# Routing per token tile, and the expert lists sorted in two unequal parts

## The chip, the cores and the metric

The kernel runs on one core of a Trainium2 chip. The metric is the device time of one execution in microseconds (us), lower is better. TensorE multiplies matrices, VectorE and ScalarE do the elementwise work, GpSimd (POOL) some of it and the indirect transfers, SyncE (SP) issues the other transfers. Each engine works through its own queue in order; semaphores join them.

## The reference

Two transformer-like blocks stand one behind the other. The change touches the end of the first and a preparation of the second. The first block's mixed features (1024 tokens x 1024) go through the output projection; the result is normalised, gated, added to the residual, normalised again to h, and h goes to a mixture of experts in which the experts choose: each of the 16 experts takes the 128 tokens (`cap`) with the highest softmax probability for it.

```python
affinity = jax.nn.softmax((h @ w_router).astype(jnp.float32), axis=-1)
gate_vals, tok_idx = lax.top_k(jnp.swapaxes(affinity, 1, 2), cap)
xs = jax.vmap(lambda hb, ib: hb[ib])(h, tok_idx)
```

Behind it the experts' gated MLPs run over `xs` and are added back to the tokens. The second block needs, among other things, columns of constants and an LRU constant (softplus of a parameter, by a series of small operations), and the keys and values of a memory of 256 tokens.

## The kernel before, in words

`first` calls `phase_out`, `phase_topk`, `setup2` and `phase_moe1`. A scheduler orders the instructions afterwards, so that pieces of these stand among each other in the engines' queues.

`phase_out` works in four blocks of two token tiles (128 tokens each). `gates(blk)` prepares a block's left factors: it loads the retention rows (`lt`), transposes them (`ltp`), loads the RWKV rows (`gy`), normalises them (`gyn`), transposes (`yT`) and gates them; high and low parts are split (`lTh`, `lTl`). The loop calls `gates` for the next block and then, for both tiles of a block, the projection (`mo`, 48 matmuls for each tile through `mm3`), a copy by ScalarE, `row_norm` (a square with a sum on ScalarE, scaling on VectorE, a power on POOL), the residual and a second `row_norm`, giving `h` (L1094, L1095), which is stored to `h2d`. `route(t, h2)` runs one tile late: 8 transpositions (`h2p`), 8 small matmuls for the logits (`rl`), a copy into a table of all tiles (`routlg`).

After the last tile one softmax over the whole table is made (L1103 to L1108), 8 matmuls against the identity (`pa`) turn it, and one copy (L1112) puts it into `affT`: 64 partitions x 512, the first 512 tokens for each expert on rows 0 to 15, the others on rows 32 to 47. `phase_topk` then runs 16 rounds of three VectorE instructions over 512 columns: the eight largest (L1127), their positions (L1128, a load of the values and a search), and their replacement by -1 (L1130). Both halves have then their 128 best in order; one merge (L1133 to L1144) keeps the larger of the first list and the reversed second one, which leaves the 128 best of all. Two transpositions (`tkps`) and two copies give the gate values `gv` and the token numbers `idx`.

`setup2` loads 88 columns of constants for the second block (`c3`, transposed through a PSUM tile), runs `phase_mem` (256 memory tokens: square, scaling, transposition `memT`, projection `mkv`, normalisation on POOL, transposition `mkT`), `lru_consts` (L1324 to L1340, 27 VectorE operations of 128x8 named `sp`, `cl`, `ncl`) and `rope_setup` (the load `posi`, its cast `posf`, the angles `ang`).

`phase_moe1` loads the weights of expert after expert in pieces of 1 MB (`m1r`), 14 of them ahead; the 15th load waits for the first gather (`xg`, an indirect transfer by `idx`, L1200). The pieces are split into `m1h` and `m1l`; the gathered tokens are transposed (`xT0p`) and multiplied (`gu`, `dn`).

## Time and profile before

| | |
|---|---|
| time, median of 3 runs | 4141.37 us (4128.83 to 4142.38) |
| profiled execution | 4133.8 us |
| its span in the trace | 4132.0 us |
| mean granted TensorE clock | 0.951 |
| PE busy | 3779.7 us (91%) |
| DVE busy | 2814.2 us (68%) |
| ACT busy | 2127.7 us (51%) |
| POOL busy | 825.2 us (20%) |

PE is TensorE, DVE VectorE, ACT ScalarE, SP SyncE. Busy shares are means over stages with different limits; the stretch of the change is read from windows and timelines, with times in us from the span's start. A granted clock of 1.00 is 2.4 GHz, 0.50 is 1.2 GHz. Durations in a row are those of one instruction, or of a run of xN instructions; L12 is line 12 of the kernel.

### The profile page before, as it was taken

Reading aid. Unit: us, or ns where it says so; the run is one execution under the profiler, and the core shown is the slowest. Engines: PE = TensorE matmul, PEld = TensorE weight load, DVE = VectorE, ACT = ScalarE, POOL = GpSimd, SP = SyncE. Lnnn points to the kernel's source line nnn. Section 1 sums busy time; section 2 is a strip of 40 time slices with the busy share of each in tenths; the row PEclk is TensorE's granted clock in tenths of the full one; section 3 lists DMA queues with packets and bytes.
Section 4 is the critical chain, followed back from the end, with each engine's and each line's share of the span. In section 5 each row is a group of like instructions: output and inputs, shape, how many; then the busy total and the mean of one; then the engine's idle time right before and its main releaser. Section 6 shows DMA issues by size and latency. Waiting matters only on the chain. (4 is left out here: it accounts for less than half of the span.)

```text
span 4132.0 us, 61749 instructions
## 1 busy us (share of the span) xinstructions
PE 3779.7 (91%) x23138; PEld 3133.2 (76%) x23138; DVE 2814.2 (68%) x4777; ACT 2127.7 (51%) x3389; POOL 825.2 (20%) x1054
## 2 busy tenths in 40 slices
PE   7988887998997879999969999999998999999998
PEld 4877886777875647777747788888886777788876
DVE  3578787776776578888865513676644356799987
ACT  3443322332323347777758712666653244688876
POOL 2333324233224120000010001222210022221111
PEclk7999998998998989999989999999999999899999
DMA  6555455455445379999851122111115425899998
GB/s 229 169 168 163 138 153 142 109 135 129 112 115 177 129 295 374 382 371 385 319 171 46 50 66 66 44 37 42 47 62 167 142 79 204 324 384 386 382 381 303
DMA packets 503961, 782.78 MB, mean 189 GB/s; under 512 B 199697, under 2 KB 334811, under 8 KB 502507
## 3 DMA queue, kind: packets, MB, share of 16 engines
q1 hardware_dynamic: 430314, 631.77, 43.8%
q0 software_dynamic: 40816, 138.37, 11.3%
q10 hardware_dynamic: 32528, 8.66, 0.9%
q8 instruction: 184, 3.01, 0.3%
q14 instruction: 119, 0.97, 0.1%
HBM read 646.28 MB, written 132.43 MB: 188 GB/s over the span
## 5 line engine op out<-in xcount | busy, mean ns | idle before, releaser
L2262 DVE TENSOR_TENSOR m2l<-m2r,m2h 128x1024 fp32r<-128x1024 f32 x380 | 449.6, 1222 | 53.0 <-ACT m2h L2261 48.6
L1195 DVE TENSOR_TENSOR m1l<-m1r,m1h 128x2048 fp32r<-128x2048 f32 x189 | 427.2, 2289 | 72.5 <-ACT m1h L1194 70.6
L2261 ACT CAST m2h<-m2r 128x1024 fp32r<-128x1024 f32 x384 | 394.0, 1050 | 86.5 <-PE m2g L109 34.6
L1194 ACT CAST m1h<-m1r 128x2048 fp32r<-128x2048 f32 x192 | 362.1, 1914 | 111.3 <-PE gu L109 82.6
L108 PE MATMUL m2g<-m2l,m2thx 128*128 128x512 f32 x512 | 202.7, 396 | 1.8 <-DVE m2l L2262 1.3
L107 PE MATMUL m2g<-m2h,m2thx 128*128 128x512 f32 x512 | 202.9, 405 | 0.3 <-ACT m2h L2261 0.3
L109 PE MATMUL m2g<-m2h,m2tlx 128*128 128x512 f32 x512 | 201.5, 394 | 0.0
L108 PE MATMUL gu<-m1l,xh 128*128 128x512 f32 x512 | 199.7, 395 | 0.0
L109 PE MATMUL gu<-m1h,xl 128*128 128x512 f32 x512 | 199.1, 395 | 0.0
L107 PE MATMUL gu<-m1h,xh 128*128 128x512 f32 x512 | 182.4, 397 | 12.7 <-ACT xh L60 8.3
L515 DVE TENSOR_TENSOR tripr<-triN,triX 128x1 f32<-128x1 f32 (+30 forms) x155 | 131.9, 851 | 19.5 <-POOL triX L511 15.9
L107 PE MATMUL apqk<-atW_hi,hT2h 128*128 128x256 f32 x512 | 145.1, 283 | 0.0
L108 PE MATMUL apqk<-atW_lo,hT2h 128*128 128x256 f32 x512 | 144.7, 283 | 0.0
L109 PE MATMUL apqk<-atW_hi,hT2l 128*128 128x256 f32 x512 | 144.7, 283 | 0.0
L107 PE MATMUL u_ps<-hTh,inW_hi 128*128 128x512 f32 (+1 forms) x336 | 127.1, 378 | 2.6 <-ACT u L342 1.5
L2314 POOL DMA_INDIRECT out_dram<-m2y,did x32 | 68.9, 2154 | 302.5 <-ACT m2y L2313 302.5
L108 PE MATMUL u_ps<-hTl,inW_hi 128*128 128x512 f32 (+1 forms) x336 | 124.4, 370 | 0.0
L109 PE MATMUL u_ps<-hTh,inW_lo 128*128 128x512 f32 (+1 forms) x336 | 124.1, 370 | 0.0
L107 PEld LDWEIGHTS gu<-m1h,xh 128*128 128x128 f32 x512 | 95.0, 188 | 37.0 <-ACT xh L60 10.7
L108 PEld LDWEIGHTS gu<-m1l,xh 128*128 128x128 f32 x512 | 96.4, 188 | 27.0 <-DVE m1l L1195 7.4
L1216 POOL DMA_INDIRECT accd<-y,idx x16 | 29.1, 1819 | 435.2 <-ACT y L1215 400.1
L108 PEld LDWEIGHTS m2g<-m2l,m2thx 128*128 128x128 f32 x512 | 96.8, 189 | 24.8 <-DVE m2l L2262 6.1
(1215 smaller groups left out, 11720.3 us busy)
## 6 DMA issues: line engine op xcount, KB each, us to landing
m2r<-in_w_gate_up_dram SPq DMA_DIRECT2D x128, 1024.0 KB
m1r<-in_w_gate_dram SPq DMA_DIRECT2D x64, 1024.0 KB
m1r<-in_w_up_dram SPq DMA_DIRECT2D x64, 1024.0 KB
m1r<-in_w_down_dram SPq DMA_DIRECT2D x64, 1024.0 KB
m2r<-in_w_down_dram SPq DMA_DIRECT2D x64, 1024.0 KB
inW_raw<-in_w_in_dram SPq DMA_DIRECT2D x72, 256.0 KB
m2w<-in_w_mod_dram POOLq DMA_DIRECT2D x32, 512.0 KB, 4.7
luW_raw<-in_w_in_dram SPq DMA_DIRECT2D x24, 512.0 KB
```

Of the source, the lines that this page charges most:

```text
L107: nc.tensor.matmul(ps, lh, rh, start=start, stop=False)
L108: nc.tensor.matmul(ps, lh, rl, start=False, stop=False)
L109: nc.tensor.matmul(ps, ll, rh, start=False, stop=stop)
L515: nc.vector.tensor_mul(pr[:, :m, :m], N[:, j, j + 1:].unsqueeze(1).to_broadcast([P, m, m]), X[:, j + 1:, j + 1:].rearrange("p s t -> p t s"))
L1194: nc.scalar.copy(hi, raw)
L1195: (nc.gpsimd if i < 3 else nc.vector).tensor_sub(lo, raw, hi)
L1216: nc.gpsimd.indirect_dma_start(out=E.accd, out_offset=bass.IndirectOffsetOnAxis(ap=E.idx[:, e:e + 1], axis=0), in_=y, in_offset=None, comp ...
L2261: nc.scalar.copy(hi, raw[:, j])
L2262: (nc.gpsimd if i in (0, 2) else nc.vector).tensor_sub(lo, raw[:, j], hi)
L2314: nc.gpsimd.indirect_dma_start(out=E.x4d, out_offset=bass.IndirectOffsetOnAxis(ap=col, axis=0), in_=y, in_offset=None, compute_op=OP.add)
```

## The change

The blocks of `phase_out` are taken in the order 1, 2, 0, 3, so that tiles 0 to 5 come first and 6 and 7 last. `route` makes the softmax of its own tile (128x16), one `pa` for the tile, and copies its 128 columns to `affA` (tiles 0 to 5, 16x768, rows 0 to 15) or `affB` (tiles 6 and 7, 16x256, rows 32 to 47). `TopK.rounds(part, n)` runs rounds of one part. Six rounds of part 0 are written behind tile 6, six ahead of tile 7's routing, four behind it, and the 16 rounds of part 1 in `phase_topk`; the replacement is made in place. The merge is as before with 768 in place of 512. The columns `c3` and `lru_consts` (now `consts2`) are called in the second block's turn of `phase_out` and use one of its PSUM tiles.

```diff
@@ -43,13 +43,13 @@
     return r
-def load_cols(E, name, srcs):
+def load_cols(E, name, srcs, psum=None):
     nc = E.nc
     n = sum(ap.shape[0] for ap in srcs)
     rows = E.misc.tile([P, P], F32, tag="colrows", name=f"{name}_rows")
     col_rows(nc, rows, srcs)
-    ps = E.ps_small.tile([P, 512], F32, tag="sm", name=f"{name}_ps")
+    ps = psum(name=f"{name}_ps") if psum else E.ps_small.tile([P, 512], F32, tag="sm", name=f"{name}_ps")
     nc.tensor.transpose(ps[:, :n], rows[:n, :], E.ident[:n, :n])
     out = E.const.tile([P, n], F32, name=name)
     nc.scalar.copy(out, ps[:, :n])
@@ -934,7 +934,8 @@
                 others.pop(0)()
-def phase_out(E, A):
+def phase_out(E, A, others, topk):
@@ -1030,7 +1031,8 @@
                     split_hl(E, zv[:, 0], lTh[:, 4 + h + 2 * q], lTl[:, 4 + h + 2 * q])
             return lTh, lTl
-        lT = [gates(0)]
+        ORDER = (1, 2, 0, 3)
+        lT = [gates(ORDER[0])]
         wo = A.w_out[0]
         rw = wo[512:1024].rearrange("(p h v) f -> p h v f", p=NPAIR, h=2)
         wts = []
@@ -1052,9 +1054,9 @@
         sh2 = bc_row(E, rp, 2, "sh2row")
         wr = rp.tile([P, KD, 16], F32, name="wrouter")
         nc.sync.dma_start(wr, A.w_router[0].rearrange("(k p) e -> p k e", p=P))
-        lg = rp.tile([P, 8, 16], F32, name="routlg")
-        lp32 = rp.tile([P, 8, 32], F32, name="routp")
-        nc.vector.memset(lp32, 0.0)
+        lps32 = [rp.tile([P, 32], F32, name=f"routp{i}") for i in range(2)]
+        for l in lps32:
+            nc.vector.memset(l, 0.0)
         def route(t, h2):
             hT = to.tile([P, KD, P], F32, tag="hT", bufs=1, name=f"h2T{t}")
@@ -1066,13 +1068,27 @@
             pl = pt.tile([P, 16], F32, tag="tr", name=f"rl{t}")
             for k in range(KD):
                 nc.tensor.matmul(pl, hT[:, k], wr[:, k], start=(k == 0), stop=(k == KD - 1))
-            nc.scalar.copy(lg[:, t], pl)
+            mx = to.tile([P, 2], F32, tag="mx", name=f"rmx{t}")
+            nc.vector.tensor_reduce(mx[:, 0:1], pl, axis=AX.X, op=OP.max)
+            g = to.tile([P, 16], F32, tag="lg", name=f"routlg{t}")
+            nc.vector.tensor_scalar(g, pl, mx[:, 0:1], None, op0=OP.subtract)
+            nc.scalar.activation(g, g, AF.Exp)
+            nc.vector.tensor_reduce(mx[:, 1:2], g, axis=AX.X, op=OP.add)
+            nc.vector.reciprocal(mx[:, 1:2], mx[:, 1:2])
+            nc.vector.tensor_scalar(lps32[t % 2][:, 0:16], g, mx[:, 1:2], None, op0=OP.mult)
+            pa = pt.tile([P, P], F32, tag="tr", name=f"pa{t}")
+            r0 = 0 if t < 6 else 32
+            nc.tensor.matmul(pa[r0:r0 + 32], lps32[t % 2], E.ident, start=True, stop=True)
+            dst = E.affA[:, t * P:(t + 1) * P] if t < 6 else E.affB[:, (t - 6) * P:(t - 5) * P]
+            nc.vector.tensor_copy(dst, pa[r0:r0 + 16])
         pend = []
-        for blk in range(4):
-            if blk < 3:
-                lT.append(gates(blk + 1))
-            lTh, lTl = lT[blk]
+        for i, blk in enumerate(ORDER):
+            if i < 3:
+                lT.append(gates(ORDER[i + 1]))
+            if i == 1:
+                others(lambda name: pt.tile([P, 512], F32, tag="tr", name=name))
+            lTh, lTl = lT[i]
             for t in (2 * blk, 2 * blk + 1):
                 sl = slice(t * P, (t + 1) * P)
                 ls = slice(t % 2 * P, (t % 2 + 1) * P)
@@ -1095,42 +1111,51 @@
                 nc.vector.tensor_add(h2, h2, sh2)
                 nc.sync.dma_start(E.h2d[sl], h2)
                 pend.append((t, h2))
-                if t:
+                if len(pend) > 1:
                     route(*pend.pop(0))
+                if t == 6:
+                    topk.rounds(0, 6)
+        topk.rounds(0, 6)
         route(*pend.pop(0))
-        pa = po.tile([64, T // 2], F32, tag="o", name="pa")
-        mx = to.tile([P, 8], F32, tag="mx", name="rmx")
-        nc.vector.tensor_reduce(mx, lg, axis=AX.X, op=OP.max)
-        nc.vector.tensor_sub(lg, lg, mx.unsqueeze(2).to_broadcast([P, 8, 16]))
-        nc.scalar.activation(lg, lg, AF.Exp)
-        nc.vector.tensor_reduce(mx, lg, axis=AX.X, op=OP.add)
-        nc.vector.reciprocal(mx, mx)
-        nc.vector.tensor_mul(lp32[:, :, 0:16], lg, mx.unsqueeze(2).to_broadcast([P, 8, 16]))
-        for t in range(8):
-            nc.tensor.matmul(pa[32 * (t // 4):32 * (t // 4) + 32, t % 4 * P:(t % 4 + 1) * P], lp32[:, t], E.ident,
-                             start=True, stop=True)
-        nc.vector.tensor_copy(E.affT, pa)
-def phase_topk(E, tp, pp):
-    nc = E.nc
-    H = T // 2
-    vals = tp.tile([64, P], F32, name="tkv")
-    ids = tp.tile([64, P], U32, name="tki")
-    b = tp.tile([64, H], F32, name="tkb")
-    cur, nxt = E.affT, b
-    for i in range(16):
-        s = slice(8 * i, 8 * i + 8)
-        nc.vector.max(vals[:, s], cur)
-        nc.vector.max_index(ids[:, s], vals[:, s], cur)
-        if i < 15:
-            nc.vector.match_replace(nxt, vals[:, s], cur, -1.0)
-            cur, nxt = nxt, cur
+        topk.rounds(0, 4)
+class TopK:
+    H = 768
+    def __init__(self, E, tp):
+        self.E, self.tp = E, tp
+        aff = tp.tile([64, self.H], F32, name="aff")
+        self.rows = [slice(0, 16), slice(32, 48)]
+        E.affA, E.affB = aff[0:16], aff[32:48, 0:T - self.H]
+        self.vals = tp.tile([64, P], F32, name="tkv")
+        self.ids = tp.tile([64, P], U32, name="tki")
+        self.cur = [E.affA, E.affB]
+        self.done = [0, 0]
+    def rounds(self, part, n):
+        nc, r = self.E.nc, self.rows[part]
+        for _ in range(n):
+            i = self.done[part]
+            self.done[part] += 1
+            cur = self.cur[part]
+            s = slice(8 * i, 8 * i + 8)
+            nc.vector.max(self.vals[r, s], cur)
+            nc.vector.max_index(self.ids[r, s], self.vals[r, s], cur)
+            if i < 15:
+                nc.vector.match_replace(cur, self.vals[r, s], cur, -1.0)
+def phase_topk(E, topk, tp, pp):
+    nc, vals, ids, H = E.nc, topk.vals, topk.ids, topk.H
+    topk.rounds(1, 16)
     idf = tp.tile([64, P], F32, name="tkf")
-    nc.vector.tensor_copy(idf, ids)
+    for r in topk.rows:
+        nc.vector.tensor_copy(idf[r], ids[r])
     v2 = tp.tile([16, P], F32, name="tkv2")
     nc.vector.tensor_copy(v2, vals[32:48, ::-1])
     i2 = tp.tile([16, P], F32, name="tki2")
@@ -2370,17 +2395,21 @@
         setattr(E, n, dt(n, [D, D]))
-def setup2(E, A, tk):
+def consts2(E, A, psum):
+    rows = lambda a: a.rearrange("(r p) -> r p", p=P)
+    E.c3 = load_cols(E, "c3", [rows(A.norm_mix_2[0]), A.conv_w_2[0].rearrange("j (r p) -> (j r) p", p=P)] +
+                     [rows(a[0]) for a in (A.conv_b_2, A.lru_ba_2, A.lru_bx_2, A.lru_lambda_2, A.norm_cx_2, A.norm_mem_2)],
+                     psum)
+    lru_consts(E)
+def setup2(E, A):
     nc, tc = E.nc, E.tc
-    rows = lambda a: a.rearrange("(r p) -> r p", p=P)
-    with tc.tile_pool(name="pssm2", bufs=1, space=PSUM) as E.ps_small:
-        E.c3 = load_cols(E, "c3", [rows(A.norm_mix_2[0]), A.conv_w_2[0].rearrange("j (r p) -> (j r) p", p=P)] +
-                         [rows(a[0]) for a in (A.conv_b_2, A.lru_ba_2, A.lru_bx_2, A.lru_lambda_2, A.norm_cx_2, A.norm_mem_2)])
     E.mkT = E.mkp.tile([P, 4, TC], F32, name="mkT")
     E.mv = E.mkp.tile([P, 2, 512], F32, name="mv")
     phase_mem(E, A)
-    lru_consts(E)
     rope_setup(E, A)
@@ -2429,11 +2458,11 @@
     E.mks = ctx.enter_context(ExitStack())
     E.mkp = E.mks.enter_context(tc.tile_pool(name="mkv", bufs=1))
     with tc.tile_pool(name="ap", bufs=1) as ap_:
-        E.affT = ap_.tile([64, T // 2], F32, name="affT")
-        phase_out(E, A)
+        topk = TopK(E, ap_)
+        phase_out(E, A, lambda psum: consts2(E, A, psum), topk)
         with tc.tile_pool(name="tkT", bufs=1) as tk, tc.tile_pool(name="tkP", bufs=1, space=PSUM) as tkp:
-            phase_topk(E, tk, tkp)
-            setup2(E, A, tk)
+            phase_topk(E, topk, tk, tkp)
+            setup2(E, A)
     phase_moe1(E, A)
```

The scheduler orders the whole anew. From the beginning of `phase_out` until about the 13th expert the queues differ; later they are the same. Three places follow.

VectorE, the first rounds, before (`affT`, `tkb`: the probabilities; `tkv`, `tki`: values and positions found; `sp`: a step of `lru_consts`):

```order
L1112 COPY affT<-pa 64x512
L1329 TENSOR_TENSOR sp_14723<-sp_14722 128x8
L1127 MAX tkv<-affT 64x8
L1332 TENSOR_TENSOR sp_14724<-sp_14724,sp_14723 128x8
L1128 MAX_INDEX tki<-tkv,affT 64x8
L1130 MATCH_REPLACE tkb<-tkv,affT 64x512
L1333 TENSOR_SCALAR sp_14724<-sp_14724 128x8
L1127 MAX tkv<-tkb 64x8
L1332 TENSOR_TENSOR sp_14724<-sp_14724,sp_14723 128x8
L1128 MAX_INDEX tki<-tkv,tkb 64x8
L1130 MATCH_REPLACE affT<-tkv,tkb 64x512
```

VectorE now, where the rounds of part 0 begin (`routp`, `pa_14443`: columns of tile 1; `h_6`: tile 6; `mix_14466`, `xr_14464`: tile 7):

```order
L1111 TENSOR_TENSOR h_6_14409<-h_6_14409,sh2row 128x1024
L1078 TENSOR_SCALAR routp_13257<-routlg_14437,rmx_14435 128x16
L1083 COPY aff<-pa_14443 16x128
L1147 MAX tkv<-aff 16x8
L1148 MAX_INDEX tki<-tkv,aff 16x8
L1150 MATCH_REPLACE aff<-tkv,aff 16x768
L1147 MAX tkv<-aff 16x8
L1148 MAX_INDEX tki<-tkv,aff 16x8
L116 TENSOR_SCALAR mx_ms<-mx_ss 128x1
L1150 MATCH_REPLACE aff<-tkv,aff 16x768
L1105 SCALAR_TENSOR_TENSOR mix_14466<-mix_14466,mx_rstd,g1row 128x1024
L1147 MAX tkv<-aff 16x8
```

VectorE now, where the columns of tile 7 are copied (`pa_14621`) and the pairs begin:

```order
L1147 MAX tkv<-aff 16x8
L1078 TENSOR_SCALAR routp_13257<-routlg_14615,rmx_14613 128x16
L1148 MAX_INDEX tki<-tkv,aff 16x8
L1083 COPY aff<-pa_14621 16x128
L1150 MATCH_REPLACE aff<-tkv,aff 16x768
L1147 MAX tkv<-aff 16x8 x2
L1148 MAX_INDEX tki<-tkv,aff 16x8 x2
L1150 MATCH_REPLACE aff<-tkv,aff 16x256
L1150 MATCH_REPLACE aff<-tkv,aff 16x768
L1147 MAX tkv<-aff 16x8 x2
L1148 MAX_INDEX tki<-tkv,aff 16x8 x2
```

The `sp` steps have left the rounds; operations of tiles 6 and 7 and their routing stand among the rounds of part 0 instead, and behind the copy rounds of both parts alternate, eight times. Behind these come eight more rounds of 256 columns, with the cast `posf` ahead of the last two.

ScalarE behind the last projection, before (`h_sq` of `xr_14332`: the square of tile 7; `memsq`, `mem`: square and scaling of the memory tokens):

```order
L127 ACTIVATE mx_sq,mx_ss<-mix_14334 128x1024
L1065 COPY h2T_14408<-h2p_14415 128x512
L1069 COPY routlg<-rl_14421 128x16
L1895 ACTIVATE memsq_14587,memss_14588<-mem_14585 128x1024
L127 ACTIVATE h_sq,h_ss<-xr_14332 128x1024
L1896 ACTIVATE memss_14588<-memss_14588 128x1
L1895 ACTIVATE memsq_14596,memss_14597<-mem_14594 128x1024
L1899 ACTIVATE mem_14585<-mem_14585,memr_14591 128x1024
```

and now (`xr_14464`: tile 7; `routlg`: the softmax of tile 6):

```order
L127 ACTIVATE mx_sq,mx_ss<-mix_14466 128x1024
L1067 COPY h2T_14540<-h2p_14547 128x512
L1920 ACTIVATE memsq_14732,memss_14733<-mem_14730 128x1024
L1921 ACTIVATE memss_14733<-memss_14733 128x1
L1924 ACTIVATE mem_14730<-mem_14730,memr_14736 128x1024
L1920 ACTIVATE memsq_14741,memss_14742<-mem_14739 128x1024
L127 ACTIVATE h_sq,h_ss<-xr_14464 128x1024
L1921 ACTIVATE memss_14742<-memss_14742 128x1
L1075 ACTIVATE routlg_14564<-routlg_14564 128x16
```

The square of tile 7 stood behind one square of memory tokens and now stands behind both squares and one scaling.

TensorE now, at the end of the projection (`pa_14443`: tile 1; `mo_7`: the last tile):

```order
L109 MATMUL mo_7_14493<-wohi_13209,lTl_13985 128x512
L107 MATMUL mo_7_14493<-wohi_13215,lTh_13984 128x512
L108 MATMUL mo_7_14493<-wolo_13216,lTh_13984 128x512
L1081 MATMUL pa_14443<-ident,routp_13257 32x128
L109 MATMUL mo_7_14493<-wohi_13215,lTl_13985 128x512
L107 MATMUL mo_7_14493<-wohi_13221,lTh_13984 128x512
```

Thirteen matmuls of the last tile stand behind this `pa`, of 28 behind the logits of its tile. For the other tiles ahead of the last block 21 to 39 matmuls stand between the logits and `pa`; before, there was none in the projection.

## Rows read from the trace of the kernel before

**Rows 1.** Windows: us, busy PE, PEld, DVE, ACT, POOL (counts), PEclk, DMA share
```profile
1270.00:1280.00 10.00, 1.71 (x4) 0.92 (x5) 6.78 (x4) 1.34 (x2) 9.55 (x5) 0.50 0.34 105
1330.00:1340.00 10.00, 10.00 (x57) 8.50 (x57) 9.55 (x15) 4.33 (x8) 3.51 (x2) 1.00 0.54 160
1430.00:1440.00 10.00, 5.10 (x33) 4.20 (x32) 2.67 (x3) 4.88 (x11) 0.54 (x1) 0.84 0.59 216
1490.00:1500.00 10.00, 0.00 (x0) 0.00 (x0) 9.76 (x27) 0.00 (x0) 0.00 (x0) 0.50 0.98 355
```

**Rows 2.** The same view, expert stage
```profile
1560.00:2040.00 480.00, 471.02 (x2140) 379.71 (x2139) 411.35 (x243) 358.75 (x269) 39.05 (x25) 1.00 1.01 377
```

**Rows 3.** Waits of PE, 1255 to 1515: total us, times, longest us
```profile
PE yT L1008 <- DVE gyn L1002: 21.9, 6, 7.4
```

**Rows 4.** Timeline of PE: start us, us, engine, line, operation, tiles, shapes, idle before
```profile
1431.70 0.39 PE L109 MATMUL mo<-wohi,lTl 128*128 128x512 f32 x1
...
1453.44 2.78 PE L1110 MATMUL pa<-ident,routp 128*32 128x128 f32 x16
...
1457.61 27.73 PE L1915 MATMUL mkv<-mew,memhT 128*128 128x512 f32 x64
...
1511.73 1.94 PE L1158 MATMUL xT0p<-ident,xg 128*128 128x128 f32 x8 [5.83 <-DMA xg<-h2d,idx]
```

**Rows 5.** Timeline of DVE, rounds of the top-k that wait for each other
```profile
1495.53 0.69 DVE L1127 MAX8 tkv<-affT 64x8 f32<-64x512 f32 x1
...
1496.33 0.68 DVE L1128 FIND_INDEX8 tki<-tkv,affT 64x8 uint32<-64x512 f32 x1
...
1497.69 0.69 DVE L1127 MAX8 tkv<-tkb 64x8 f32<-64x512 f32 x1
```

**Rows 6.** Timeline of DVE, round with small operations between, and one stalled
```profile
1459.13 0.69 DVE L1127 MAX8 tkv<-tkb 64x8 f32<-64x512 f32 x1
1459.74 0.14 DVE L1332 TENSOR_TENSOR sp<-sp,sp 128x8 f32<-128x8 f32 x1
...
1459.93 0.68 DVE L1128 FIND_INDEX8 tki<-tkv,tkb 64x8 uint32<-64x512 f32 x1
...
1467.67 4.19 DVE L1333 TENSOR_SCALAR sp<-sp 128x8 f32<-128x8 f32 x1
```

**Rows 7.** DVE by line and shape, 1390 to 1504: busy us, mean ns
```profile
L1333 DVE TENSOR_SCALAR sp<-sp 128x8 f32<-128x8 f32 x9 | 9.2, 1019 | 0.0
L1332 DVE TENSOR_TENSOR sp<-sp,sp 128x8 f32<-128x8 f32 x9 | 6.4, 707 | 0.0
...
L1095 DVE TENSOR_TENSOR h<-h,sh2row 128x1024 f32<-128x1024 f32 x4 | 4.9, 1225 | 0.1
```

**Rows 8.** Timeline of DVE, tile 6, end of the routing, end of the top-k
```profile
1427.00 1.22 DVE L1095 TENSOR_TENSOR h<-h,sh2row 128x1024 f32<-128x1024 f32 x1
...
1456.25 0.68 DVE L1112 COPY affT<-pa 64x512 f32<-64x512 f32 x1 [1.71 <-PE pa L1110]
...
1502.81 0.68 DVE L1128 FIND_INDEX8 tki<-tkv,tkb 64x8 uint32<-64x512 f32 x1
1503.52 0.21 DVE L1135 COPY tkv<-tkv 16x128 f32<-16x128 f32 x1
1503.77 0.22 DVE L1133 CAST tkf<-tki 64x128 f32<-64x128 uint32 x1
1503.91 0.27 DVE L1140 TENSOR_TENSOR tkm<-tkv,tkv 16x128 f32<-16x128 f32 x1
...
1506.04 0.17 DVE L1149 CAST idx<-tkps 128x16 int32<-128x16 f32 x1
```

**Rows 9.** Timeline of ACT behind the last tile's projection
```profile
1438.95 1.04 ACT L127 ACTIVATE h_sq<-xr 128x1024 f32<-128x1024 f32 x1
...
1441.12 1.13 ACT L1899 ACTIVATE mem<-mem,memr 128x1024 f32<-128x1024 f32 x1
```

**Rows 10.** Timeline of SP's queue
```profile
1488.72 0.37 SPq L1452 DMA_DIRECT2D posi<-in_positions_dram  x1
```

## The prediction

> **What bounds the kernel now.** I read the windows first. In the expert stage TensorE is busy 471 of 480 us at the full clock [rows 2]; it starts when the tokens of expert 0 are gathered, and from there the program's order is unchanged, so what the change is worth is the shift of that gather, one to one. Next the timeline and waits of the stretch before it. The last matmul of the output projection (mo) starts at 1431.70, the gathered tokens are transposed (xT0p) at 1511.73, after a wait of 5.83 us for the gather's DMA [rows 4]. In between stands VectorE: routing ends with the copy of affT at 1456.25, the index lists are cast (idx) at 1506.04 [rows 8]. From 1490 to 1500 TensorE does nothing at all and VectorE is busy 9.76 of 10 us [rows 1]. So the 49 us from the copy to idx are the bound, and the end of that copy is set by tile 7 alone. What has to be seen is how much VectorE work lies ahead of idx, and from when it can run.
>
> **Prices.** A round of the top-k on 512 columns takes 2.16 us from MAX8 to MAX8 [rows 5]. No row has another width, so I take the slope between MAX8 on 512 columns, 0.69 us, and an addition on 1024, 1.225 us [rows 5, 7]: 1.05 ns a column. A round has three passes, so 768 columns cost 2.16 + 3 x 256 x 1.05 ns = 2.97 us and 256 columns 1.35 us. Sixteen rounds were 34.6 us and become 69. The rows also show why the old stretch is longer than its rounds: the small "sp" operations (lru_consts) cost nothing where they stand free (FIND_INDEX8 starts 0.80 us after MAX8 with one between them and without [rows 5, 6]), but some take up to 4.19 us [rows 6]; the 18 in the two groups sum to 15.6 us [rows 7], where 18 x 0.14 would be 2.5. So 13 us of the old stretch are stalls of sp, and these leave it.
>
> **The sum, part by part.** (1) *Start.* Part 0 needs the six middle and first tiles, the last of them tile 1; its columns' scaling stands on VectorE right behind h of tile 6. That addition ends in the kernel before at 1428.2 [rows 8]. Scaling, the matmul pa and the copy follow: 1.0 us, an estimate from the 0.14 us of a small operation [rows 6] and 0.68 us for a copy four times as wide [rows 8]. The earlier pa matmuls push the projection back: the sixteen for eight tiles took 2.78 us [rows 4] while the clock was low, say 0.17 us a tile at full clock, 1.0 us for six. Part 0 starts at about 1430.2. Hence hardly any round is beside the projection, which ends 2 us later; what the rounds can use is the time of tile 7's norms, where VectorE was busy 2.67 of 10 us [rows 1].
>
> (2) *Until tile 7's columns are copied.* VectorE's queue has eight rounds of part 0 there, the last replacement behind the copy. I take 2.85 us a round (0.08 us of overlap at some borders, as in rows 6): 8 x 2.85 - 0.95 = 21.9. Among them stand four operations of 128x1024 for tile 7, 4 x 1.225 = 4.9 [rows 7], and fourteen small ones, 1.8 [rows 6]. ScalarE now squares tile 7 (h_sq) behind the scaling of the memory tokens and their second square; it ran at 1438.95, ahead of both, and each takes about 1.1 [rows 9], so it comes some 3 us later; VectorE's own queue reaches that point at about 1443, so I add 0.8 of stall. Sum 29.4: the copy ends at 1459.6, against 1456.9 before, **2.7 us later**.
>
> (3) *From there to idx.* Eight pairs (a round of part 0, a round of part 1), 8 x (2.97 + 1.35) = 34.6; eight rounds of part 1 alone, less one replacement, 10.4; operations for the rotary tables 0.8; the merge, which took from the end of the last FIND_INDEX8 (1503.49) to idx 2.55 [rows 8]. 48.4 us, against 49.1: **0.7 us less**. The doubled rounds eat the 13 us of stalls. If neighbours in a pair overlapped by 0.08 us at six borders, a pair would be 3.84 and idx 3.8 us earlier. I don't take it: at the merge the COPY that begins at row 32 starts 0.03 us after its predecessor's end, and the CAST behind it, back at row 0, 0.04 after that COPY's end, where the next addition starts 0.08 before the CAST ends [rows 8]. Parts 0 and 1 lie on rows 0 and 32 and alternate.
>
> The Trainium skill ("VectorE: DVE Perf Modes", section "Two Vector instructions with no wait between them") speaks against the change here: an instruction whose operands start in another group of 32 partitions than the previous ones' starts only when every earlier Vector instruction has finished. These rows agree; by that rule pairs cost 4.32 us, without it idx would lie about 2 us before the old one, not after.
>
> (4) *Hidden.* The sp operations and c3 move into the second block's turn: 27 small operations, 0 to 3.8 us at 0.14 each [rows 6], where VectorE is busy 9.55 of 10 us in one window [rows 1] but the projection covers what follows; I take nothing. The table of memory keys now starts behind tile 7's copy: from its first matmul (mkv, 1457.61) to the load of positions (posi, 1488.72) took 31.1 us [rows 4, 10]. With even 8 us of transpositions ahead, posi is issued at 1459.6 + 8 + 31.1 = 1498.7, while the cast that waits for it on VectorE (posf, now ahead of the last two rounds) is reached at about 1502. Three megabyte loads stand behind posi instead of five, so the queue should be empty again for the gather, which ran against 0.98 of the DMA engines until 1500 [rows 1]. If this cover goes, every us of the memory table is a us of the end.
>
> **Sum.** +2.7 - 0.7 = +2.0 us: 4135.8 against the profiled execution's 4133.8. That one lies 7.6 below the median of the three runs; the four executions have their middle at 4137.6, so I forecast 4140. Bounds: all rounds at 2.73 and pairs overlapped, 5 less; no overlap anywhere, and h_sq's 3 us in full, 4 more; the four executions spread by -9 to +5. So the forecast's own range is 4127 to 4149. A difference under 0.3%, 12.4 us, is no change here.
>
> **Rivals.**
> *Faster: the front.* TensorE waits six times for gyn (the normalised rows of a block's gates), 21.9 us in all, longest 7.4 [rows 3]; around 1270 it works 1.71 of 10 us at a clock of 0.50 [rows 1]. If with block 1 first the gates are ready when asked for, and the projection ends about 16 us earlier, everything follows: +2 - 16 = -14, **4124**. For it: the change's first gates no longer wait for the last-written rows. Against it: VectorE at 9.55 of 10 in 1330 to 1340 [rows 1] paces the middle, so time gained at the front is likely waited for there. 17%.
>
> *Slower: pa in TensorE's queue.* Each tile's pa stands 20 to 40 matmuls behind its logits and waits for a chain of five VectorE operations and an Exp. Where each stands behind a 128x1024 operation of 1.2 us [rows 7], the chain takes 5 x 1.4 + 1 = 8 us, against 5 to 9 us of matmuls in front (21 to 39 of them at 0.22, which is 471 us over 2140 [rows 2]). It decides when the chain is longer than these: then the projection stops in each tile, 2 to 3 us six times, and all that follows moves. 16 more: **4156**. For it: the full window above; against it: from 1430 to 1440 VectorE had 7.33 us free, and its load falls toward the end. 19%.
>
> *The change doesn't do what it says*: rounds beside the projection. By (1) that is so in my forecast already.
>
> **How the numbers follow.** No change 64% (4140). Faster by over 0.3%: 17%; slower: 19%. The range takes in most of both rivals: 4122 to 4157.
>
> **What would show it.** In the changed profile: MAX8 on 768 columns near 0.95 us and on 256 near 0.42; a pair near 4.3 us; part 0's first MAX8 at about 1430, tile 7's copy near 1460, idx near 1508; no sp beside the rounds; posf without a wait. I am wrong if mo ends more than 5 us from 1432, if pa waits in TensorE's list of waits for more than 1 us each, if posf is waited for, or if rounds cost other than by width.

## The result and the profile after

The change made the kernel slower: 4156.2 us (median of 7, 4144.6 to 4169.4) against 4136.6 (median of 7), a ratio of 1.0051 with an interval of 1.0029 to 1.0073. A second measurement of the same kernel gave 4158.8 and 1.0067 (1.0049 to 1.0086). I had forecast 4140 and given slower 19%.

The profiled execution of the changed kernel, 4169.2 us, is one of the two slowest of its runs; where that comes from has to be seen before its rows are read. First the timeline of TensorE in the changed kernel, at five places: the last matmul of the retention scan (y), the first and the last of the output projection (mo), and two transpositions, of the gathered tokens of expert 0 (xT0p) and of the hidden activations of expert 15 (hT15p):

```profile
1245.55 0.56 PE L916 MATMUL y<-vt,pm 128*128 128x64 f32 x4
...
1281.04 1.22 PE L107 MATMUL mo<-wohi,lTh 128*128 128x512 f32 x2 [4.29 <-ACT wohi L1049]
...
1450.01 0.39 PE L109 MATMUL mo<-wohi,lTl 128*128 128x512 f32 x1
...
1538.12 1.94 PE L1183 MATMUL xT0p<-ident,xg 128*128 128x128 f32 x8 [6.05 <-DMA xg<-h2d,idx]
...
2099.35 0.93 PE L1183 MATMUL hT15p<-ident,hh 128*128 128x128 f32 x7
```

And the rows of the kernel before for the first, the second and the last of these (the others: [rows 4]):

```profile
1230.53 0.56 PE L916 MATMUL y<-vt,pm 128*128 128x64 f32 x4
...
1268.45 1.22 PE L107 MATMUL mo<-wohi,lTh 128*128 128x512 f32 x2 [5.21 <-ACT wohi L1047]
...
2070.69 0.93 PE L1158 MATMUL hT15p<-ident,hh 128*128 128x128 f32 x7
```

At the end of the scan the changed kernel is already 15.0 us late, though everything up to there is the same code in the same order. The second profile of it reaches the same point (the last y of such a row: 1230.8 before, 1245.8 here) at 1223.0, 7.8 us ahead of the kernel before. So those 15 us are chance, and I count from the scan's end (the start of its last y). Then (changed against before): the first mo comes 2.4 us earlier (35.5 against 37.9), the last mo 3.3 later, expert 0 11.4 later, expert 15 13.6 later, the end of the program 20.3 later; in the second profile the last two are 10.3 and 19.8. The experts thus carry on what they are given, and the rest is in the second block (below).

VectorE in the changed kernel, where part 0 begins, around the copy of tile 7's columns, the first pair of rounds, and the end:

```profile
1447.21 0.28 DVE L1083 COPY aff<-pa 16x128 f32<-16x128 f32 x1 [0.78 <-PE pa L1081]
1447.53 0.95 DVE L1147 MAX8 tkv<-aff 16x8 f32<-16x768 f32 x1
...
1461.42 0.15 DVE L116 TENSOR_SCALAR h_ms<-h_ss 128x1 f32<-128x1 f32 x1 [1.57 <-ACT h_sq L127]
...
1474.14 0.17 DVE L1072 TENSOR_REDUCE rmx<-rl 128x1 f32<-128x16 f32 x1 [1.80 <-PE rl L1070]
...
1479.37 0.28 DVE L1083 COPY aff<-pa 16x128 f32<-16x128 f32 x1
...
1480.66 1.40 DVE L1147 MAX8 tkv<-aff 16x8 f32<-16x256 f32 x2
...
1482.18 0.42 DVE L1148 FIND_INDEX8 tki<-tkv,aff 16x8 uint32<-16x256 f32 x1
...
1482.72 0.95 DVE L1148 FIND_INDEX8 tki<-tkv,aff 16x8 uint32<-16x768 f32 x1
...
1483.80 0.41 DVE L1150 MATCH_REPLACE8 aff<-tkv,aff 16x256 f32<-16x256 f32 x1
...
1484.33 0.94 DVE L1150 MATCH_REPLACE8 aff<-tkv,aff 16x768 f32<-16x768 f32 x1
1485.30 1.40 DVE L1147 MAX8 tkv<-aff 16x8 f32<-16x256 f32 x2
...
1516.98 0.42 DVE L1147 MAX8 tkv<-aff 16x8 f32<-16x256 f32 x1
...
1517.51 0.41 DVE L1148 FIND_INDEX8 tki<-tkv,aff 16x8 uint32<-16x256 f32 x1
1517.96 0.08 DVE L1150 MATCH_VALUE_LOAD aff<-tkv,aff 16x8 f32 x1
...
1518.47 0.42 DVE L1147 MAX8 tkv<-aff 16x8 f32<-16x256 f32 x1
...
1525.45 0.40 DVE L1150 MATCH_REPLACE8 aff<-tkv,aff 16x256 f32<-16x256 f32 x1
1525.88 0.17 DVE L1479 CAST posf<-posi 128x8 f32<-128x8 int32 x1
...
1532.22 0.17 DVE L1174 CAST idx<-tkps 128x16 int32<-128x16 f32 x1
```

The widths cost what was forecast: 0.95 us for 768 columns, 0.42 for 256. With the 0.69 us of 512 columns on 64 rows [rows 5] the three lie on one line: 16 rows cost as much as 64, and the two parts are twice the rounds. Part 0 starts at 1447.5, tile 7's copy ends at 1479.7, the pair from 1480.66 to 1485.30 takes 4.64, idx starts at 1532.2, where it stood at 1506.0 [rows 8]; posf waits for nothing. Two stalls stand in this stretch: h_ms for the square of tile 7, 1.57, and rmx for tile 7's logits, 1.80.

A round of part 1 alone takes 1.48 us (1516.98 to 1518.47). One border in it has changed against the kernel before, where the replacement goes into another table (tkb) and its load of values (MATCH_VALUE_LOAD) starts 0.08 us before FIND_INDEX8 ends at 1497.01 [rows 5]:

```profile
1496.93 0.06 DVE L1130 MATCH_VALUE_LOAD tkb<-tkv,affT 64x8 f32 x1
```

Now the replacement is made in place, and the load starts 0.04 us behind that end (1517.96 against 1517.92). That the replacement in place is the reason is read from these rows; no run changes it alone.

The waits of TensorE between 1250 and 1540 in the changed kernel (total us, times, longest):

```profile
PE yT L1009 <- DVE gyn L1003: 24.5, 7, 8.2
...
PE pa L1081 <- DVE routp L1078: 18.8, 3, 14.0
...
PE h2p L1066 <- DVE aff L1083: 2.3, 1, 2.3
```

and three of its eight pa in the timeline:

```profile
1351.99 0.38 PE L1081 MATMUL pa<-ident,routp 128*32 128x128 f32 x2 [0.32 <-DVE routp L1078]
...
1468.18 0.61 PE L1081 MATMUL pa<-ident,routp 128*32 128x128 f32 x2 [14.02 <-DVE routp L1078]
...
1478.55 0.61 PE L1081 MATMUL pa<-ident,routp 128*32 128x128 f32 x2 [4.45 <-DVE routp L1078]
```

The six pa inside the projection wait 0.3 us in all; the two long waits are those of the last tiles, behind it. The wait that is new inside the projection is that of h2p, the next transposition, for the copy of pa's result (aff). The waits for gyn [rows 3] are no shorter with the new order of blocks.

### The profile page after: what moved, and what is told of

The parts are those of the page before. It is cut to its first block, busy times and chain, and to the rows that moved or that the text cites. A ratio compares the mean times of both kernels' runs of the same rounds, so it can differ in the third digit from the quotient of the medians.

```text
span 4167.3 us, 61861 instructions
## 1 busy us (share of the span) xinstructions
PE 3798.5 (91%) x23138; PEld 3145.2 (75%) x23138; DVE 2842.8 (68%) x4899; ACT 2130.8 (51%) x3388; POOL 825.2 (20%) x1054
## 3 DMA queue, kind: packets, MB, share of 16 engines
q0 software_dynamic: 40816, 138.37, 11.3%
## 5 line engine op out<-in xcount | busy, mean ns | idle before, releaser
L107 PE MATMUL gu<-m1h,xh 128*128 128x512 f32 x512 | 185.6, 398 | 12.6 <-ACT xh L60 9.8
L1657 DVE TENSOR_SCALAR_CACHE_REDUCE pr<-sc 128x512 f32<-128x512 f32 (+2 forms) x192 | 103.6, 551 | 17.0 <-PE sc L1653 14.4
```

Of the source, the lines that this page charges most:

```text
L107: nc.tensor.matmul(ps, lh, rh, start=start, stop=False)
L1657: nc.vector.tensor_scalar(pr[:, m, n0:n1], ps[m][:, :n], -1.0, None, op0=OP.mult, op1=OP.min, accum_out=s[:, 4 * i + m:4 * i + m + 1])
```

## The experiments

All stretches are from the profiles, one for each kernel, in us: scan's end to idx, and within it the projection (first to last mo), last mo to the end of the last copy of probabilities, and that copy to idx; "gather" runs from idx to the transposition xT0p.

| kernel | time, ratio (95%) | projection | to copy | to idx | gather | scan's end to idx |
|---|---|---|---|---|---|---|
| before | 4136.6 | 163.2 | 25.2 | 49.1 | 5.7 | 275.2 |
| changed | 4156.2, 1.0051 | 169.0 | 29.6 | 52.6 | 5.9 | 286.4 |
| consts | 4121.8, 0.9967 (0.9955 to 0.9979) | 161.1 | 23.6 | 36.5 | 9.1 | 256.4 |
| posi | 4116.1, 0.9949 (0.9930 to 0.9968) | 159.8 | 24.2 | 36.5 | 5.8 | 255.8 |
| unconsts | 4150.0, 1.0030 (1.0017 to 1.0043) | 166.9 | 29.8 | 56.8 | 5.8 | 288.7 |
| rows0 | 4140.9, 1.0010 (0.9996 to 1.0024) | 172.6 | 29.6 | 44.1 | 5.7 | 282.3 |
| late2 | 4171.8, 1.0085 (1.0064 to 1.0105) | 168.9 | 20.7 | 75.3 | 5.8 | 299.2 |
| order | 4154.0, 1.0045 (1.0030 to 1.0059) | 168.7 | 29.8 | 52.6 | 5.6 | 287.1 |
| tiles | 4136.5, 0.9995 (0.9982 to 1.0008) | 174.9 | 20.9 | 37.0 | 9.7 | 269.9 |
| nopa | 4126.0, 0.9985 (0.9974 to 0.9996) | 163.0 | 22.3 | 36.5 | 9.2 | 258.3 |
| palate | 4131.4, 0.9993 (0.9981 to 1.0004) | 172.5 | 20.8 | 37.3 | 9.4 | 266.5 |
| pagate | 4126.6, 0.9972 (0.9960 to 0.9984) | 164.3 | 20.7 | 37.2 | 9.3 | 259.2 |
| mended | 4137.0, 0.9992 (0.9978 to 1.0006) | 163.9 | 28.2 | 45.7 | 5.6 | 272.4 |

Ratios go against the runs of the kernel before in the same batch (medians 4133 to 4137). In the last column two profiles of the same kernel differ by 0.7 us (before) and 1.1 (changed).

**consts: only the moved constants.** The kernel before, with `c3` and `lru_consts` called in the second block's turn.

```diff
             if blk < 3:
                 lT.append(gates(blk + 1))
+            if blk == 1:
+                others(lambda name: pt.tile([P, 512], F32, tag="tr", name=name))
...
```

> The kernel before with one part of the change alone: the columns c3 and lru_consts are called in the second block's turn of phase_out; routing and top-k stay as they were. Theory 1 (the small sp operations cost the top-k 13 us of stalls behind POOL, and nothing else there decides): idx comes 10 to 13 us earlier after the copy of affT than the 49.1 us of before, about 37, and the time is 10 to 13 us below the kernel before. Rival (the stalls pass to other instructions, or the gather then waits for the memory table or the load queue): copy to idx shorter, but the wait of xT0p grows by as much, time within 3 us of before.

The old rounds without sp among them take 36.5 us in place of 49.1: 12.6 us of stalls are gone, as the sum had it, and the projection does not pay for the move. Part of that is lost again at once: xT0p now waits 9.2 us for its gather. On SP's queue posi, which needs a buffer that the memory table gives back, is issued at 1483.34, and the weight loads behind it then stand ahead of the gather.

The wait in consts (TensorE's list of waits) and posi on SP's timeline:

```profile
PE xT0p L1160 <- DMA xg<-h2d,idx: 9.2, 1, 9.2
```

```profile
1483.34 0.37 SPq L1454 DMA_DIRECT2D posi<-in_positions_dram  x1
```

**posi: consts, and the loads posi and invf in buffers of their own.**

```diff
-        pi = tp.tile([P, 8], I32, name="posi")
+        pi = E.tk.tile([P, 8], I32, name="posi")
...
-        fr = tp.tile([P, 8], F32, name="invf")
+        fr = E.tk.tile([P, 8], F32, name="invf")
...
```

> The kernel 'consts' with the tiles of positions and frequencies in the pool of the top-k, so that their loads don't wait for the memory table and don't hold the weight loads behind them. Theory 1 (in consts the gather stands behind weight loads that were held until 1483, and xT0p waits 9.2 us where 5.8 would do): 14 weight loads are through before the gather, xT0p waits about 6 us, time about 3 us below consts, 4118 to 4120. Rival (without the hole all weight loads are queued ahead of the gather all the same): xT0p waits 9 us or more, time as consts.

The same two views of posi:

```profile
PE xT0p L1160 <- DMA xg<-h2d,idx: 5.9, 1, 5.9
```

```profile
1445.64 1.53 SPq L1454 DMA_DIRECT2D posi<-in_positions_dram  x1
```

Counted from the scan's end, posi is issued 43 us earlier, and the gather's wait is short again. This kernel is the best of all: 0.9949, 40 us under the changed one, 20 under the one before.

**unconsts: the change with the constants back where they were.**

```diff
-            if i == 1:
-                others(lambda name: pt.tile([P, 512], F32, tag="tr", name=name))
...
     phase_mem(E, A)
+    lru_consts(E)
```

> The changed kernel with c3 and lru_consts back in setup2. Theory 1 (the small operations among the rounds are held behind POOL's wide ones, and each also breaks between partition groups): copy of tile 7 to idx grows from 52.6 us by 8 to 14, time 8 to 14 us above the changed kernel, 4164 to 4170. Rival (the doubled rounds leave POOL's wide operations room, the stalls fall elsewhere): within 4 us of the changed kernel.

A miss: among the doubled rounds the sp operations cost 4.2 us (56.8 against 52.6), not 12.6, and the time, 4150.0, is not above the changed kernel's. What the constants are worth depends on what they stand among.

**rows0: both parts on rows 0 to 15**, in tables of their own.

```diff
-            r0 = 0 if t < 6 else 32
+            r0 = 0
...
-        aff = tp.tile([64, self.H], F32, name="aff")
...
-        E.affA, E.affB = aff[0:16], aff[32:48, 0:T - self.H]
+        E.affA = tp.tile([16, self.H], F32, name="affA")
+        E.affB = tp.tile([16, T - self.H], F32, name="affB")
...
```

> The changed kernel with part 1 of the top-k on partitions 0 to 15, like part 0, in tiles of its own; same rounds, same widths. Theory 1 (an instruction that starts in another group of partitions than its predecessors is held until they end): a pair of rounds falls from 4.64 us to about 3.9, copy of tile 7 to idx from 52.6 to about 46 us, time 5 to 7 us below the changed kernel. Rival (the gaps come from the pairs of instructions, a value load and a search, whatever the partitions): pairs stay at 4.6, no difference.

VectorE in rows0, the first pair, and the cast of posf:

```profile
1467.05 0.41 DVE L1146 MAX8 tkv<-affB 16x8 f32<-16x256 f32 x1
1467.38 0.93 DVE L1146 MAX8 tkv<-affA 16x8 f32<-16x768 f32 x1
...
1468.30 0.41 DVE L1147 FIND_INDEX8 tki<-tkv,affB 16x8 uint32<-16x256 f32 x1
...
1468.70 0.94 DVE L1147 FIND_INDEX8 tki<-tkv,affA 16x8 uint32<-16x768 f32 x1
...
1469.62 0.40 DVE L1149 MATCH_REPLACE8 affB<-tkv,affB 16x256 f32<-16x256 f32 x1
...
1470.02 0.93 DVE L1149 MATCH_REPLACE8 affA<-tkv,affA 16x768 f32<-16x768 f32 x1
1470.88 0.40 DVE L1146 MAX8 tkv<-affB 16x8 f32<-16x256 f32 x1
...
1505.74 0.42 DVE L1146 MAX8 tkv<-affB 16x8 f32<-16x256 f32 x1
1506.09 0.14 DVE L1480 CAST posf<-posi 128x8 f32<-128x8 int32 x1
```

A pair takes 3.83 us (1467.05 to 1470.88), as I had worked out for overlapped neighbours, against 4.64: each instruction starts about 0.07 us before the one ahead of it ends, where in the changed kernel it starts 0.02 to 0.03 behind that end and its load of values does not overlap either. The stretch shrinks by 8.5 us, 6.4 of them in the eight pairs; a round of part 1 alone is 1.48 us here too. rows0 gives the parts tables of their own as well, but posf, whose tiles are the same in both kernels, points to the rows: it starts 0.03 us behind the end of its predecessor on row 32 in the changed kernel (1525.88 against 1525.85), and 0.07 before the end of its predecessor on row 0 here. The rule that the prediction cited from the Trainium skill ("VectorE: DVE Perf Modes", section "Two Vector instructions with no wait between them") is what these rows show, and the price here is 0.81 us for the six borders of a pair. The time falls by 15 us where 5 to 7 were expected; from the scan's end to idx it is 4.1 (the projection is 3.6 longer), and the rest is not explained.

**late and late2: no rounds ahead of the last copy.** late drops the early calls and writes all rounds in `phase_topk`.

```diff
-                if t == 6:
-                    topk.rounds(0, 6)
-        topk.rounds(0, 6)
         route(*pend.pop(0))
-        topk.rounds(0, 4)
...
+    topk.rounds(0, 16)
     topk.rounds(1, 16)
```

> The changed kernel with no round ahead of the last tile's routing: all 16 rounds of both parts stand in phase_topk. Theory 1 (VectorE's work behind the projection is the bound): the eight rounds of part 0 that ran earlier, about 23 us, come behind the last copy, which itself comes about 10 us earlier since nothing stands in the way of tile 7's routing; idx and time about 10 to 13 us later than the changed kernel. Rival (the early rounds delay the routing by as much as they take): within 3 us of the changed kernel.

No test: the scheduler drew the rounds forward by itself, and seven of part 0 began ahead of the copy (to copy 26.6, to idx 57.8, 4155.4 us; the expectation of late2 counts eight). late2 forbids it, by an edge from the last copy to the first round:

```diff
-            nc.vector.tensor_copy(dst, pa[r0:r0 + 16])
+            E.last_aff = nc.vector.tensor_copy(dst, pa[r0:r0 + 16])
...
-            nc.vector.max(self.vals[r, s], cur)
+            m = nc.vector.max(self.vals[r, s], cur)
+            if part == 0 and i == 0:
+                load_after(self.E, m, self.E.last_aff)
```

> The changed kernel with a dependency that keeps the first round of part 0 behind the copy of tile 7's columns, so that no round runs earlier (in 'late' the scheduler had put eight of them back). Theory 1 (eight rounds run ahead of the copy at the price of a later copy): the copy comes 8 to 11 us earlier after the end of the scan, sixteen pairs of 4.64 us follow, copy to idx about 78 us, idx 13 to 17 us later, time 13 to 17 us above the changed kernel. Rival (the early rounds delay the copy by what they take, 23 us): the copy comes 20 us earlier and the time is within 4 us of the changed kernel.

VectorE in late2, the last copy and two pairs:

```profile
1457.67 0.28 DVE L1083 COPY aff<-pa 16x128 f32<-16x128 f32 x1 [0.79 <-PE pa L1081]
1457.99 1.40 DVE L1143 MAX8 tkv<-aff 16x8 f32<-16x768 f32 x2
...
1462.64 1.40 DVE L1143 MAX8 tkv<-aff 16x8 f32<-16x768 f32 x2
```

With nothing in its way the last copy comes 20.7 us behind the last mo, and all 16 pairs, 4.64 or 4.65 each, follow: 75.3 us. So the eight rounds drawn forward in the changed kernel save 22.7 us behind the copy and delay the copy by 8.9.

**order: the blocks in their old order**, ORDER = (0, 1, 2, 3).

```diff
-        ORDER = (1, 2, 0, 3)
+        ORDER = (0, 1, 2, 3)
```

> The changed kernel with the blocks in the old order 0, 1, 2, 3 (tiles 0 to 5 still first). Theory 1 (the tail decides, the order of the blocks is worth little): the end of the projection, counted from the last step of the RWKV scan, moves by under 3 us, time within 4 us of the changed kernel. Rival (the new order stalls the projection): the projection ends 5 to 10 us earlier and the time falls by as much.

Projection 168.7, as in the changed kernel (169.0 and 168.7); the time is the same too. The order of the blocks gives nothing and costs nothing, and the faster rival falls with it.

**tiles, nopa, palate, pagate: what lengthens the projection.** tiles is consts with the routing of each tile (softmax, pa, copy) from the change, and the old top-k.

```diff
+            pa = pt.tile([P, P], F32, tag="tr", name=f"pa{t}")
+            r0 = 32 * (t // 4)
+            nc.tensor.matmul(pa[r0:r0 + 32], lps32[t % 2], E.ident, start=True, stop=True)
+            nc.vector.tensor_copy(E.affT[r0:r0 + 32, t % 4 * P:(t % 4 + 1) * P], pa[r0:r0 + 32])
...
```

> The kernel 'consts' with one more part of the change: routing per tile (softmax, pa and copy for each tile), the top-k still 16 rounds on 64x512 after the last copy. Theory 1 (the split of the top-k is what costs, per-tile routing is hidden by the projection): end of the projection within 2 us of consts, last copy up to 4 us earlier, copy to idx 36 to 37 us, time 4117 to 4123. Rival (per-tile routing stalls TensorE and VectorE in the projection, the slower rival of the prediction): projection ends 5 us or more later than in consts, time 4128 or more.

The projection takes 174.9 us against 161.1, and the time rises by 14.8. nopa is tiles with the softmax of each tile, but the eight pa and one copy at the end:

```diff
-            pa = pt.tile([P, P], F32, tag="tr", name=f"pa{t}")
...
+        for t in range(8):
+            nc.tensor.matmul(pa[32 * (t // 4):32 * (t // 4) + 32, t % 4 * P:(t % 4 + 1) * P], lp32[:, t], E.ident,
+                             start=True, stop=True)
```

> The kernel 'tiles' (consts, routing per tile, top-k as before) with the eight matmuls pa and their one copy behind the last tile's routing; the softmax itself is still made tile by tile. Theory 1 (what lengthens the projection is pa in TensorE's queue, with its PSUM tile): the projection, first to last mo, comes back from 175 us in tiles to 160 to 164 as in consts; time 4120 to 4125. Rival (the small VectorE and ScalarE operations of the softmax, in the queues ahead of the gates' operations, lengthen it): 170 us or more, time as tiles, 4136.

163.0: it is pa with its copy, not the 40 small operations of the softmax. palate writes each pa one tile later, so that its softmax is long done:

```diff
                 if t:
+                    if t > 1:
+                        turn(t - 2)
                     route(*pend.pop(0))
...
```

> The kernel 'tiles' with pa and the copy of a tile one tile later, ahead of the next tile's transpositions. Theory 1 (pa waits in TensorE's queue for a chain that isn't through yet): a tile later the chain is long through, projection 160 to 165 us, time 4120 to 4126. Rival (the work itself, or the PSUM tile that pa takes from the transpositions, is what costs): projection 170 us or more, time 4133 or more.

172.5: it is not the wait for the softmax either; in tiles no pa inside the projection waits for it. pagate leaves pa where it is in the program and takes its PSUM tile from the pool of the gates instead of "tr", whose two tiles `ltp`, `h2p`, `rl` and pa share:

```diff
-            pa = pt.tile([P, P], F32, tag="tr", name=f"pa{t}")
+            pa = pg.tile([P, 2, 256], F32, tag="gate", name=f"pa{t}")[:, 0, 0:P]
```

> The kernel 'tiles' with pa in a PSUM tile of the gates' pool instead of the two tiles that the transpositions and the logits share. Theory 1 (the shared PSUM tile is what costs: from the logits through the softmax to the copy of pa it is taken from the transpositions of the next gates and of h2p): projection 161 to 166 us, no wait of h2p for the copy of pa, time 4121 to 4127. Rival (pa in TensorE's in-order queue costs, wherever its result goes): projection 170 us or more, time 4131 or more.

164.3. The pool does not change alone: the scheduler makes another order for TensorE from it. In tiles the eight ltp of the next block and the h2p of the next tile stand behind the first pa (pa at 1337.02, ltp from 1337.36, h2p at 1340.97), in pagate ahead of it (ltp from 1335.31, h2p at 1345.74, pa at 1346.98). What pagate shows is that the shared pair of tiles costs; how much of it by this order and how much by waits is not separated.

TensorE in tiles, around the pa of the second tile (timeline):

```profile
1361.67 0.41 PE L1079 MATMUL pa<-ident,routp 128*32 128x128 f32 x2
1362.01 0.66 PE L1064 MATMUL h2p<-ident,h 128*128 128x128 f32 x4
...
1365.41 0.66 PE L1064 MATMUL h2p<-ident,h 128*128 128x128 f32 x4 [2.31 <-DVE affT L1080]
```

Half of the next transposition goes at once; the other half needs the tile that pa holds and waits 2.31 us until VectorE has copied it. In pagate that wait is gone, and one of 4.8 us in two pieces stands at the gates' matmul (gp); the projection is shorter all the same:

```profile
PE gp L1012 <- DVE affT L1080: 4.8, 2, 2.8
```

The direct wait is 2.3 of the 14 us. The windows of tiles and of posi over the third to the fifth tile of the projection, 72.5 against 63.4 us (busy PE, PEld, DVE, ACT, POOL, then the granted clock), show 9 us more:

```profile
1318.50:1391.00 72.50, 62.85 (x306) 50.68 (x304) 51.32 (x126) 29.89 (x58) 24.01 (x18) 0.90 0.39 123
```

```profile
1326.60:1390.00 63.40, 55.87 (x297) 45.85 (x296) 51.82 (x112) 27.94 (x56) 24.76 (x18) 0.97 0.44 141
```

TensorE is idle 9.7 us in tiles and 7.5 in posi; the other 7 us are busy time, at a granted clock of 0.90 against 0.97: the clock alone, 55.87 x 0.97 / 0.90, makes 4.3 of them. That the new gaps bring the lower clock is argued from these rows, not shown.

Another 4 us are in the sixth tile, and these are not pa's. There TensorE runs without a gap in both tiles and the run order (above), whose TensorE queue has the same order there; first tiles, then order:

```profile
1390.80:1409.60 18.80, 18.80 (x76) 15.38 (x75) 8.61 (x19) 3.98 (x10) 1.08 (x2) 0.74 0.21 70
```

```profile
1397.70:1412.10 14.40, 14.40 (x77) 11.58 (x75) 8.80 (x20) 4.17 (x10) 1.08 (x2) 1.00 0.27 98
```

The granted clock is 0.74 in tiles, so about half of the stretch at 1.2 GHz, and 1.00 in order; ahead of it both had waited 3.1 us for gyn, and the rows don't tell why one falls and the other doesn't. rows0, palate and nopa have the slow sixth tile too, and nopa has no pa there; both profiles of the changed kernel are without it. Less these 4 us, tiles loses some 6 us against pagate, not 10.6, and palate stands at about 168. The times are less sharp than the profiles: the intervals of tiles, nopa and palate overlap, and that of pagate touches that of tiles.

**mended: the changed kernel with rows0, pagate and posi**.

```diff
-            pa = pt.tile([P, P], F32, tag="tr", name=f"pa{t}")
-            r0 = 0 if t < 6 else 32
+            pa = pg.tile([P, 2, 256], F32, tag="gate", name=f"pa{t}")[:, 0, 0:P]
+            r0 = 0
...
-        pi = tp.tile([P, 8], I32, name="posi")
+        pi = E.tk.tile([P, 8], I32, name="posi")
...
```

> The changed kernel with three mends: part 1 on partitions 0 to 15 (as rows0), pa in the gates' PSUM pool (as pagate), and the loads of positions free of the memory table (as posi). Theory 1 (held pairs and the shared PSUM tile are what the change lost beside its doubled rounds): projection 161 to 166 us, copy to idx 44 us, idx about 78 to 82 us behind the last mo, time 4130 to 4137, still 14 us or more above posi, because sixteen wide and sixteen narrow rounds are more work than sixteen of 512 columns. Rival (the split pays once mended): within 5 us of posi, 4116 to 4121.

4137.0 us, as before the change, and 21 above posi. The projection is back at 163.9 (169.0 in the changed kernel, 172.6 with the slow sixth tile in rows0), so the shared PSUM tile costs in the split kernel too, some 5 us. From the scan's end to idx 16.5 us are left against posi: 9.2 behind the copy and 4.0 ahead of it, where 32 rounds of 16 rows stand in place of 16 rounds of 64, and 4.1 in the projection (the first mo is 0.7 earlier). posi with pagate's routing wasn't tried.

**after2 and before2: the two kernels once more**, unchanged (no diff), for the spread.

> The changed kernel once more, unchanged. Theory 1 (the 15 us by which its profile is late at 1190 us already, in a part of the program whose order the change leaves alone, are chance): the profile reaches the end of the scan at 1226 to 1240, time 4145 to 4160. Rival (something of the change slows the early part, by the places of its tiles): 1243 or later again, time 4165 or more.

> The kernel before once more, unchanged, for a second profile. Theory 1: the end of the scan between 1226 and 1246, the projection from first to last mo within 4 us of the first profile's 163, and from there to idx within 1 us of 74.3. Rival (the front differs from run to run as much as between the kernels): projection off by 8 us or more.

From the scan's end to the program's end: 2921.5 and 2921.0 us for the changed kernel, 2901.2 and 2903.1 for the one before. What lies behind the scan repeats within 2 us, what lies ahead of it (1245.8, 1223.0; 1230.8, 1226.3) does not; the 1223.0 is even earlier than expected.

## Why the prediction was wrong

Forecast at idx: +2.0 us. Measured from the scan's end: +11.2 there, and +20 at the end of the program. Term by term, with the 15.0 us of the early part taken off the changed profile:

- *Start of part 0*: 1430.2 forecast, 1432.5 measured. **This is the first step that failed**: the projection was to pay 1.0 us for the pa matmuls and pays 5.8 (169.0 against 163.2). The place was that of my slower rival, pa in TensorE's queue, but not its mechanism: I had pa wait for its softmax, and the six waited 0.3 us in all. The lengthening goes with the shared PSUM tile (163.9 in mended), which I had not looked at. That part 0 starts only 2.3 late is due to the first mo, which came 2.4 earlier.
- *To the copy*: 29.4 forecast, 32.1 measured. The stall at h_sq was there, 1.57 in place of 0.8, and one I didn't have, 1.80 for the logits of tile 7; they make 2.6 of the 2.7.
- *Copy to idx*: 48.4 forecast, 52.6 measured. **The second step that failed, in size**: the pair at 4.32 us was 4.64, eight times (2.6), and a round of part 1 alone 1.48 in place of 1.35, eight times (1.0). I had counted no overlap between neighbours of a pair, which was right, but took both prices from old rounds, where the replacement's load still overlaps; 1.48 stands in rows0 too, so it is no matter of the rows but, by the rows above, of the replacement in place. The widths themselves were right.
- *The stalls of sp*: 13 us forecast, 12.6 measured alone (consts). The move itself cost nothing, as said. That the gather then meets posi and the weight loads shows only without the split (consts: 9.2); in the changed kernel it is 6.0.
- *posf*: not waited for, as forecast.
- *Behind idx, one to one*: right for the experts (+11.4 at expert 0, +13.6 and +10.3 at expert 15 in the two profiles), **not for the end: the third step that failed**, and its cause stays open. Behind expert 15, where the order is unchanged, the changed kernel loses 6.7 and 9.5 us more against the first profile of before; but the second profile of before loses 2.9 there too, consts and posi, which are faster, lose 5.8 and 4.8, and over all sixteen profiles this stretch takes 2061 to 2072 us. The medians speak against mere chance: changed, late, late2 and order are 7 to 12 us slower than the shift of their gather, unconsts and rows0 within 1 us of it.

Of the prediction's signs of being wrong, mo's end stayed away (3.3 us late), the two long waits of pa stand behind the projection and not in it, and the rounds did cost other than by width. Of the rivals, slower was priced at 4156 and came out at 4156.2 by luck: 16 us were to come from the projection, and 6 did.

The account against before at idx, from the experiments one at a time (an estimate, since they were not all measured in the same company): stalls of sp -12.6; 16 rounds as 16 wide and 16 narrow with borders +38.8 (late2 less posi); eight rounds ahead of the copy -22.7 + 8.9; softmax by tile -4.5 (25.2 to 20.7); projection +5.8; earlier first mo -2.4: together +11.3. The runs in between cancel, so that the sum is bound to come out; it orders the parts and tests none of them, and unconsts shows that the first is worth less beside doubled rounds.

## What to carry to other kernels

Splitting a chain of dependent passes so that half of it can start early pays only if the half is short: here it doubled the work at the end, and the waiting time that it could use was 14 us net. Before a small step is moved into an engine's full stretch, look at what buffers it takes, not only at what it waits for: eight 32x128 results in a double-buffered PSUM tag, with matmuls of about 0.4 us each, cost the projection some 5 us (changed against mended). And a change made of several parts is tried part by part: one here was worth 13 us alone, 20 with two loads in buffers of their own, and the rest took more than that back.

## What the runs showed of the hardware

The same instructions in the same order take 1223 to 1246 us up to the scan's end from run to run. TensorE's windows from 700 to 750 us, before and changed:

```profile
700.00:750.00 50.00, 41.31 (x440) 30.58 (x440) 38.18 (x104) 16.08 (x35) 22.56 (x29) 0.90 0.54 136
```

```profile
700.00:750.00 50.00, 42.47 (x340) 30.08 (x338) 30.42 (x70) 13.20 (x27) 23.84 (x30) 0.64 0.52 122
```

The granted clock is 0.90 in the one and 0.64 in the other, and 100 matmuls fewer are done. A profile that lies 15 us late has to be read from a common point, not from the span's start.
